# Moving norm sums from TensorE to GpSimd, and one residual stream from TensorE transposes to VectorE squares and GpSimd copies

## The chip, the core and the metric

The kernel runs on one core of a Trainium2 chip. A core has five engines with queues of their own: TensorE (PE in the profile, its weight loads PEld), VectorE (DVE), ScalarE (ACT), GpSimd (POOL) and SyncE (SP), which here issues DMAs. Each engine works through its own queue in order, and waits on semaphores for what others make. The metric is the device time of one execution in microseconds, as the median of the runs. Before the change it is 1138.27 us (three runs, 1137.84 to 1138.35).

## The reference, cut to what matters

A trunk of four pre-norm residual layers over 256 tokens of width 1024, in float32. Layers 0 and 3 mix tokens by differential attention, layer 1 by block attention (with 256 tokens a single causal block), layer 2 by windowed attention with sinks. Each is followed by a squared-ReLU feed-forward of width 4096, and the end is one more norm.

```
h = x
for i in range(4):
    h = h + mixer_i(rms_norm(h, attn_norm_g[i]))
    a = rms_norm(h, mlp_norm_g[i])
    h = h + (maximum(a @ w_up[i], 0) ** 2) @ w_down[i]
return rms_norm(h, final_norm_g)

rms_norm(x, g) = x * rsqrt(mean(x * x) + 1e-6) * g
```

The mean runs over the 1024 features of a token. A factor per token can be pulled out of every product that follows: the kernel multiplies by the gain `g` early and by the root later. For a mixer the factor is `rsqrt(mean)`. For the feed-forward the square of the ReLU turns it into `1 / mean`, which is multiplied in after the down projection.

## The kernel before, in words

The residual stream lies transposed in SBUF: four tiles `hT[j]` of 128 features x 512 (two blocks of 128 features, each with 256 tokens). A float32 product is made of float32r pieces: each operand is split into a high part and a remainder (`whi` by ScalarE, `wlo` by VectorE, L189 and L190; `hg`, `uu`, `oo` in the same way), and three of the four products are added in PSUM. The weights come as 185 pieces of 128x2048, fetched by SyncE up to five pieces ahead and split two pieces ahead of TensorE (`take`). So VectorE's subtraction for a piece stands in its queue between the other work, some two pieces before TensorE needs it.

PSUM has eight banks, four with the tag `wk` (`p_up`, `p_sum`, `p_row`, scores, transposes) and four with `acc` (`p_in`, `p_d`, `p_down`, `p_res`, `p_last`). A group of the up projection (`up_proj`, 16 groups a layer) fills two `wk` banks; VectorE joins each with ScalarE's copy `cross` (L742) and frees it, and the group after next writes it again.

A norm's sum of squares is gathered as the stream is updated: `norm_sum` squares each `hT[j]` on ScalarE and adds on VectorE, which gives `acc`, 128 partitions x 256 tokens (L359). What is left is a sum over the 128 partitions, and TensorE does it with a matrix of ones, in two forms:

- `mean_square` (`p_sum`, L368): `acc` is the stationary operand, so the result has tokens on partitions. It serves the four mixers, through `norm_factor` and the Newton steps of `rsqrt`, whose result `nr` scales the products out of PSUM (L713 for queries and keys), and the last feed-forward, as `factor`.
- `mean_row` (`p_row`, L383): the ones are stationary, so every partition holds all 256 token sums. VectorE scales it to `rowx` and takes the reciprocal into `row` (L948). It serves the feed-forwards of layers 0 to 2, whose down projection leaves features on partitions (`into`, L753).

In the last layer the output must have tokens on partitions. So after group 1 of the up projection (`then`) TensorE transposes the whole stream, 16 blocks of 128x128 into `p_res`, and ScalarE copies it to `res[t]`, 128 tokens x 1024 (L961). `down_out` makes the last down projection in two halves of 512 columns, adds `res` (`close`, L853), and scales by the final norm (`finish`); GpSimd raises to the power -0.5 there (L321).

The order on each engine is made by a planner that lists instructions as it expects them to become ready; on TensorE some instructions are held behind others by hand (`TURNS`: in layers 1 and 3 the first `p_sum` stands behind the 32nd `p_in`). A reader of a result stands at a fixed place in its engine's queue; if the result is late, all that is behind it is late too.

Of the kernel before, what the change touches and what calls it, by code (L numbers as in the profile page):

```python
# [4 lines left out]

# [5 lines left out]

F32 = mybir.dt.float32
F32R = mybir.dt.float32r
I32 = mybir.dt.int32
AF = mybir.ActivationFunctionType
OP = mybir.AluOpType
AX = mybir.AxisListType

P = 128
D = 1024  # L20
S = 256
NT = S // P
# [3 lines left out]
EPS = 1e-6  # L26
# [34 lines left out]
        (("p_s", 16), ("p_in", 168)),  # L61
    ),
    1: (
        (("p_sum", 0), ("p_in", 31)),
        (("p_s", 0), ("p_in", 83)),
        (("p_s", 12), ("p_in", 131)),
        (("p_s", 24), ("p_in", 227)),
# [20 lines left out]
        (("p_d", 150), ("p_d", 161)),  # L88
    ),
    3: (  # L90
        (("p_sum", 0), ("p_in", 31)),
        (("p_s", 0), ("p_in", 83)),
        (("p_s", 12), ("p_in", 131)),
        (("p_s", 24), ("p_in", 225)),
# [52 lines left out]
def trunk(ctx: ExitStack, tc: tile.TileContext, xT, gains, lams, swa_row, fng, weights, out):  # L147
# [8 lines left out]
    def bank(tag, name):  # L156
        return ps.tile([P, 512], F32, tag=tag, name=name, bufs=4)

    def room(j, shape, name, dt=F32):

        return sb.tile(shape, dt, tag=f"slot{j}", name=name, bufs=1)
# [36 lines left out]
    def take():  # L198
        i = used[0]
        used[0] += 1  # L200
        while len(fetched) < min(weights.shape[0], i + FAR + 1):
            fetch()
        while len(staged) < min(weights.shape[0], i + LOOK + 1):
            stage()
        return staged[i]

    def r3(n):
        return lambda t: t.rearrange("p (a b) -> p a b", a=n)
# [153 lines left out]
    def mean_square(n):  # L362

        p = bank("wk", "p_sum")
        for t in range(NT):
            T.matmul(p[:, P * t:P * t + P], n.acc[:, P * t:P * t + P], ones, start=True, stop=True)
        x = tiny.tile([P, NT], F32, tag="nx", name="nx", bufs=1)
        V.tensor_scalar(x, p[:, :S].rearrange("p (t m) -> p t m", m=P)[:, :, 0], 1.0 / D, EPS, op0=OP.mult, op1=OP.add)  # L368
        return x

    def norm_factor(n, by_power):

        x = mean_square(n)
        r = tiny.tile([P, NT], F32, tag="nr", name="nr")
        rsqrt(r, x, NT, by_power)
        return r

    def mean_row(n):

        p = bank("wk", "p_row")  # L380
        T.matmul(p[:, :S], ones, n.acc, start=True, stop=True)
        x = sb.tile([P, S], F32, tag="rowx", name="rowx", bufs=1)
        V.tensor_scalar(x, p[:, :S], 1.0 / D, EPS, op0=OP.mult, op1=OP.add)  # L383
        return x

    def mm3(out, lh, ll, rh, rl, start, stop, **kw):
# [216 lines left out]

    def mixer_layer(i, n):
        mixer, slot = i % 3, i // 3
        r = norm_factor(n, i == 0)
        parts = []
        kpad = new_keys()
        if mixer == 2:
# [223 lines left out]
                    block_step(p, hi[:, k], lo[:, k], us[16 * h + k], h + k == 0, h == 1 and k == 15)  # L833
            into(n, d, p, row)

    def down_out(us, res, factor):

        grow = sb.tile([P, D], F32, tag="raw", name="grow", bufs=RAW)
        nc.sync.dma_start(grow, bcast(fng, D))
        ss = cst.tile([P, 2, NT], F32, name="fss")  # L840
        x = cst.tile([P, 2, NT], F32, name="fx")
        r = cst.tile([P, NT], F32, name="fr")


        given = [sb.tile([P, D], F32, tag=f"hg{t}", name=f"given{t}", bufs=1) for t in range(NT)]

        def close(t, p, c, part, first=0):


            width = p.shape[-1]  # L850
            o, s = slice(t, t + 1), slice(512 * c + first, 512 * c + first + width)
            y = res[t][:, s]
            V.scalar_tensor_tensor(y, p, factor[:, o], y, op0=OP.mult, op1=OP.add)  # L853
            if part is None:
                return
            sq = sb.tile([P, 512], F32, tag="relu", name="sq")
            if s.stop == D:
                V.tensor_tensor_reduce(sq[:, :width], y, y, op0=OP.mult, op1=OP.add, scale=1.0 / D,
                                       scalar=x[:, 0, o], accum_out=x[:, 1, o])
                return  # L860
            A.activation(sq[:, :width], y, AF.Square, accum_out=ss[:, part, o])
            V.tensor_tensor(given[t][:, s], y, grow[:, s], op=OP.mult)

        def finish(t, bound, fresh):

            o = slice(t, t + 1)
            y = r[:, o]
            rsqrt(y, x[:, 1, o], 1, True)
            rows = slice(P * t, P * t + P)
            z = given[t]  # L870
            A.activation(z[:, :bound], z[:, :bound], AF.Copy, scale=y)
            nc.scalar.dma_start(out[rows, :bound], z[:, :bound])
            if bound < fresh:
                s = slice(bound, fresh)
                V.tensor_scalar(z[:, s], z[:, s], y, None, op0=OP.mult)
                nc.sync.dma_start(out[rows, s], z[:, s])
            s = slice(fresh, D)
            V.scalar_tensor_tensor(z[:, s], res[t][:, s], y, grow[:, s], op0=OP.mult, op1=OP.mult)
            nc.sync.dma_start(out[rows, s], z[:, s])

        def sofar(t, parts):
            o = slice(t, t + 1)
            V.tensor_scalar(x[:, 0, o], ss[:, 0, o], 1.0 / D, EPS, op0=OP.mult, op1=OP.add)
            for j in parts:
                V.scalar_tensor_tensor(x[:, 0, o], ss[:, j, o], 1.0 / D, x[:, 0, o], op0=OP.mult, op1=OP.add)

        for c in range(2):
            banks = [bank("acc", "p_last") for _ in range(NT)]
            parts = []

            def last(t, ks, p=None, first=0, alone=False):
                p = banks[t] if p is None else p
                cols = slice(first, first + p.shape[-1])
                for q, k in ks:
                    hi, lo = parts[q]
                    u, s = us[4 * q + k], slice(P * t, P * t + P)
                    mm3(p, u[:, 0, s], u[:, 1, s], hi[:, k, cols], lo[:, k, cols],
                        (q, k) == (ks[0] if alone else (0, 0)), (q, k) == ks[-1] and k == 3 and q > 5,
                        skip_group_check=True)

            for q in range(8):
                parts.append([r3(4)(x) for x in take()])
                if q < 6:
                    for k in range(4):
                        for t in range(NT):
                            last(t, [(q, k)])
            ends = [(q, k) for q in (6, 7) for k in range(4)]
            last(0, ends)
            close(0, banks[0], c, c)
            if c == 0:  # L910
                last(1, ends)
                close(1, banks[1], 0, 0)
                for t in range(NT):
                    sofar(t, [])
            else:
                finish(0, 512, 512)

                last(1, ends[:4])
                close(1, banks[1], 1, None)
                for h in range(2):  # L920
                    p = bank("acc", "p_last")[:, :256]
                    last(1, ends[4:], p, 256 * h, True)
                    close(1, p, 1, 1 + h, 256 * h)
                    if h == 0:
                        sofar(1, [1])
                finish(1, 448, 768)
# [9 lines left out]
    for i in range(DEPTH):  # L936
        T.layer = i
        parts, rest = mixer_layer(i, n)
        n = new_norm(gv[:, 1, i, :])
        (out_proj if i % 3 == 1 else out_proj_all)(parts, n, rest)  # L940
        held = {}

        def then(g):
            if i + 1 < DEPTH:
                if g == 1:
                    x = mean_row(n)
                    held["row"] = sb.tile([P, S], F32, tag="row", name="row", bufs=1)
                    V.reciprocal(held["row"], x)  # L948
            elif g == 1:
                held["factor"] = cst.tile([P, NT], F32, name="factor")  # L950
                V.reciprocal(held["factor"], mean_square(n))

                held["res"] = [room(16 + t, [P, D], f"res{t}") for t in range(NT)]
                for j in range(4):
                    p = bank("acc", "p_res")
                    for t in range(NT):
                        for b in range(2):
                            T.transpose(p[:, S * t + P * b:S * t + P * b + P],
                                        hT[j][:, S * b + P * t:S * b + P * t + P], ident)
                    for t in range(NT):  # L960
                        A.activation(held["res"][t][:, S * j:S * j + S], p[:, S * t:S * t + S], AF.Copy)  # L961

        us = up_proj(n, then)
        if i + 1 < DEPTH:
            n = new_norm(gv[:, 0, i + 1, :])
            down_proj(us, n, held["row"])
        else:
            down_out(us, held["res"], held["factor"])
    T.take_turns(tc)


# [76 lines left out]
```

## Time and profile before

| what | value |
|---|---|
| median of three runs | 1138.27 us |
| profiled execution | 1137.97 us, its span 1136.2 us |
| granted TensorE clock | 0.999 |
| TensorE busy | 1128.4 us, 99% |
| VectorE busy | 826.2 us, 73% |
| ScalarE busy | 659.8 us, 58% |
| GpSimd busy | 13.2 us, 1%, 43 instructions |
| HBM read | 196.52 MB, 174 GB/s over the span |
| last up projection, last down projection | about 950.6 to 1042.5 us, from there to 1129.7 us |

How to read the rows. A row of a timeline has the start in microseconds, the duration, the engine, the line of the kernel, the operation, the tiles written and read (out<-in), the shape and, after x, how many like instructions are merged in the row; in brackets stands how long the engine was idle before it and what ended that. Matmuls overlap in TensorE's pipeline, so a matmul of 0.40 us may start 0.24 us after the one ahead of it: what one costs is the step between starts. A float32 matmul appears as two instructions. The chain of waits goes back from the last instruction to whatever released each step.

### The profile page before, as it was taken

How to read it: one execution, taken by the hardware profiler on the slowest of the kernel's cores; microseconds unless marked ns; L12 is line 12 of the kernel's file. 1: busy time of each engine (PE TensorE's matmuls, PEld its weight loads, DVE VectorE, ACT ScalarE, POOL GpSimd, SP SyncE). 2: the span in 40 equal slices, each digit the busy share in tenths (PEclk: the TensorE clock that was granted, in tenths of full speed). 3: DMA queues.
4: the chain of work that ended last, by engine and by line, in shares of the span. 5: the costliest groups of instructions: out<-in, count | busy, mean ns of one | idle time of the engine just before them, and what ended most of it. 6: DMA issues, size and time to landing. Idle time of an engine off the chain costs nothing.

```text
span 1136.2 us, 17013 instructions
## 1 busy us (share of the span) xinstructions
PE 1128.4 (99%) x6556; PEld 984.3 (87%) x6556; DVE 826.2 (73%) x1586; ACT 659.8 (58%) x1203; POOL 13.2 (1%) x43
## 2 busy tenths in 40 slices
PE   9999999999999999999999999999999999999997
PEld 7889888888888888888899998888888899888886
DVE  8888977656677697776569887765667788777453
ACT  7766666544476666654446765554446767565342
POOL 2000000000000000000000000000000000000000
PEclk9999999999999999999999999999999999999999
DMA  8543555555544345555553346555554434554551
GB/s 332 197 149 116 185 201 194 194 186 186 185 149 148 122 176 200 196 197 186 185 209 112 112 153 218 185 186 190 190 198 140 145 140 166 196 194 168 186 185 37
DMA packets 30464, 198.66 MB, mean 175 GB/s; under 512 B 3504, under 2 KB 5040, under 8 KB 7216
## 3 DMA queue, kind: packets, MB, share of 16 engines
q1 hardware_dynamic: 30096, 197.09, 50.1%
q8 instruction: 51, 0.84, 0.3%
q10 hardware_dynamic: 288, 0.49, 0.1%
q14 instruction: 29, 0.24, 0.1%
HBM read 196.52 MB, written 1.05 MB: 174 GB/s over the span
## 4 chain that ended last, share of the span: by engine, by line
PE 97%; ACT 1%; DVE 1%; issue 0%; DMA 0%; SPq 0%; POOLq 0%; POOL 0%; DVEq 0%
PE p_up L129 31%; PE p_down L129 23%; PE p_in L129 19%; PE p_last L129 7%; PE p_d L129 7%; PE p_s L129 3%; PE p_av L129 2%; PE p_t L132 1%; PE p_qk L132 1%; PE p_e L129 1%; DMA raw<-in_weights 0%; PE p_o L132 0%; ACT whi L189 0%; ACT hg L345 0%; PE p_sum L129 0%
## 5 line engine op out<-in xcount | busy, mean ns | idle before, releaser
L190 DVE TENSOR_TENSOR wlo<-raw,whi 128x1024 fp32r<-128x1024 f32 (+1 forms) x374 | 446.2, 1209 | 198.2 <-ACT whi L189 197.8
L189 ACT ACTIVATE whi<-raw 128x1024 fp32r<-128x1024 f32 (+1 forms) x374 | 383.9, 1046 | 203.5 <-issue 113.9
L129 PE MATMUL p_up<-hg,whi 128*128 128x512 f32 x1024 | 356.2, 394 | 0.0
L129 PE MATMUL p_up<-hg,wlo 128*128 128x256 f32 x1024 | 283.1, 277 | 0.0
L129 PE MATMUL p_down<-uu,whi 128*128 128x512 f32 x768 | 266.4, 394 | 0.0
L129 PEld LDWEIGHTS p_up<-hg,whi 128*128 128x128 f32 x1024 | 191.8, 188 | 44.0
L129 PE MATMUL p_in<-whi,hg 128*128 128x512 f32 (+1 forms) x736 | 213.3, 372 | 0.0
L129 PE MATMUL p_down<-uu,wlo 128*128 128x256 f32 x768 | 212.7, 277 | 0.0
L129 PEld LDWEIGHTS p_up<-hg,wlo 128*128 128x128 f32 x1024 | 192.3, 188 | 0.5
L129 PEld LDWEIGHTS p_down<-uu,whi 128*128 128x128 f32 x768 | 144.0, 188 | 33.4
L129 PEld LDWEIGHTS p_in<-whi,hg 128*128 128x128 f32 x736 | 132.8, 189 | 22.7 <-ACT hg L345 0.4
L129 PEld LDWEIGHTS p_down<-uu,wlo 128*128 128x128 f32 x768 | 144.2, 188 | 0.0
L129 PE MATMUL p_in<-wlo,hg 128*128 128x512 f32 (+1 forms) x368 | 130.1, 368 | 0.1
L129 PE MATMUL p_d<-oo,whi 128*128 128x256 f32 (+1 forms) x416 | 85.5, 296 | 0.0
L821 ACT ACTIVATE uu<-u 128x512 fp32r<-128x512 f32 x64 | 40.5, 632 | 73.4 <-DVE u L819 73.4
L129 PE MATMUL p_last<-whi,uu 128*128 128x512 f32 (+1 forms) x264 | 79.3, 383 | 0.0
L129 PEld LDWEIGHTS p_in<-wlo,hg 128*128 128x128 f32 x368 | 68.9, 189 | 11.5 <-DVE wlo L190 0.5
L741 ACT ACTIVATE cross<-p_up 128x256 f32<-128x256 f32 x128 | 48.0, 375 | 37.4 <-PE p_up L129 35.4
L129 PEld LDWEIGHTS p_d<-oo,whi 128*128 128x128 f32 x416 | 66.5, 191 | 2.1 <-issue 0.2
L345 ACT ACTIVATE hg<-hT,gn 128x256 fp32r<-128x256 f32 x64 | 31.4, 503 | 61.3 <-DVE hT L754 60.9
L456 ACT ACTIVATE e<-ns,nm 128x128 f32<-128x128 f32 (+1 forms) x128 | 56.8, 446 | 13.3 <-DVE nm L453 13.3
L129 PE MATMUL p_d<-oo,wlo 128*128 128x256 f32 x224 | 63.7, 285 | 0.0
(170 smaller groups left out, 1069.4 us busy)
## 6 DMA issues: line engine op xcount, KB each, us to landing
raw<-in_weights SPq DMA_DIRECT2D x181, 1024.0 KB, 4.9
raw<-in_weights SPq DMA_DIRECT2D x8, 256.0 KB, 4.7
raw<-in_weights SPq DMA_DIRECT2D x4, 512.0 KB, 7.2
hT<-in_xT SPq DMA_DIRECT2D x8, 128.0 KB, 4.6
bias<-in_swa_row SPq DMA_DIRECT2D x1, 512.0 KB, 4.3
grow<-in_fng SPq DMA_DIRECT2D x1, 512.0 KB, 3.4
lv<-in_lams SPq DMA_DIRECT2D x1, 256.0 KB, 6.0
out<-given ACTq DMA_DIRECT2D x1, 256.0 KB, 2.8
```

The source lines that it names most:

```text
L129: return self.keep(out.tensor.name.rstrip("_0123456789"), self.engine.matmul(out, *args, **kw))
L132: return self.keep(out.tensor.name.rstrip("_0123456789"), self.engine.transpose(out, *args, **kw))
L189: high = A.activation(hi[:, s], raw[:, s], AF.Copy)
L190: low = V.tensor_tensor(lo[:, s], raw[:, s], f(hi[:, s]), op=OP.subtract)
L345: A.activation(both[:, 0], h, AF.Copy, scale=g)
L456: A.activation(e[:, s], ns[:, s], AF.Exp, bias=nm[:, t:t + 1], scale=-1.0, accum_out=l[:, t:t + 1])
L741: A.activation(cross, p[:, S:], AF.Copy)
L821: A.activation(both[:, :, 0], r3(2)(u), AF.Copy)
```

## The change

Three things are changed.

1. Where `mean_row` and two of the mixers (layers 1 and 3), and the last feed-forward, had a matmul with ones, GpSimd now sums `acc` over the partitions (`partition_all_reduce`); every partition gets all 256 sums. `mean_row` scales that row in place. Where tokens must be on partitions (`mean_column`), VectorE multiplies each 128x128 half of the row with the identity and sums along the row, which picks each partition's own token. The mixers of layers 0 and 2 keep the matmul. The two entries of `TURNS` that placed `p_sum` go.
2. The 16 transposes of the last layer and ScalarE's eight copies go. Instead VectorE transposes `hT` in squares of 32x32 (`turn_stream`, one instruction for each of the four tiles), and GpSimd puts the squares in place with 64 copies of 32 partitions x 128 elements. This stands behind the second and third piece of the last down projection's first half; the buffers `hg2` and `hg3` hold the squares.
3. `res` is made in `down_out` and is no longer handed to it.

In the built program TensorE's order is otherwise the same. GpSimd has two more instructions without operands, ahead of the first sum over partitions and of the last powers.

```diff
-    def norm_factor(n, by_power):
-        x = mean_square(n)
+    def norm_factor(n, by_power, direct):
+        x = mean_square(n) if direct else mean_column(n)
...
+    def sum_row(n):
+        x = sb.tile([P, S], F32, tag="row", name="row", bufs=1)
+        G.partition_all_reduce(x, n.acc, P, ROP.add)
+        return x
+
     def mean_row(n):
-        p = bank("wk", "p_row")
-        T.matmul(p[:, :S], ones, n.acc, start=True, stop=True)
-        x = sb.tile([P, S], F32, tag="rowx", name="rowx", bufs=1)
-        V.tensor_scalar(x, p[:, :S], 1.0 / D, EPS, op0=OP.mult, op1=OP.add)
+        x = sum_row(n)
+        V.tensor_scalar(x, x, 1.0 / D, EPS, op0=OP.mult, op1=OP.add)
+        return x
+
+    def mean_column(n):
+        row = sum_row(n)
+        x = tiny.tile([P, NT], F32, tag="nx", name="nx", bufs=1)
+        for t in range(NT):
+            junk = sb.tile([P, P], F32, tag="junk", name="junk", bufs=1)
+            V.tensor_tensor_reduce(junk, row[:, P * t:P * t + P], ident, op0=OP.mult, op1=OP.add, scale=1.0 / D,
+                                   scalar=EPS, accum_out=x[:, t:t + 1])
         return x
...
-        r = norm_factor(n, i == 0)
+        r = norm_factor(n, i == 0, mixer != 1 and i < 3)
...
+        res = [room(16 + t, [P, D], f"res{t}") for t in range(NT)]
+        def turn_stream(j):
+            z = sb.tile([P, 2, 2, NT, 4, 32], F32, tag=f"hg{2 + j}", name=f"squares{j}", bufs=1)
+            for h in range(2):
+                V.transpose(z[:, h].rearrange("p a t i c -> p (a t i c)"), hT[2 * j + h])
+            for t in range(NT):
+                for i in range(4):
+                    for g in range(4):
+                        to = res[t][32 * i:32 * i + 32, 512 * j:512 * j + 512]
+                        G.tensor_copy(to.rearrange("p (a b c) -> p a b c", a=4, c=32)[:, :, g, :],
+                                      z[32 * g:32 * g + 32].rearrange("p h a t i c -> p (h a) t i c")[:, :, t, i, :])
...
+                if c == 0 and q in (1, 2):
+                    turn_stream(q - 1)
...
-                    x = mean_row(n)
-                    held["row"] = sb.tile([P, S], F32, tag="row", name="row", bufs=1)
-                    V.reciprocal(held["row"], x)
+                    held["row"] = mean_row(n)
+                    V.reciprocal(held["row"], held["row"])
...
-                V.reciprocal(held["factor"], mean_square(n))
-                held["res"] = [room(16 + t, [P, D], f"res{t}") for t in range(NT)]
-                for j in range(4):
-                    p = bank("acc", "p_res")
-                    for t in range(NT):
-                        for b in range(2):
-                            T.transpose(p[:, S * t + P * b:S * t + P * b + P],
-                                        hT[j][:, S * b + P * t:S * b + P * t + P], ident)
-                    for t in range(NT):
-                        A.activation(held["res"][t][:, S * j:S * j + S], p[:, S * t:S * t + S], AF.Copy)
+                V.reciprocal(held["factor"], mean_column(n))
```

More of the change, by code (lines that the diff above doesn't have):

```diff
@@ L7 @@
 import concourse.tile as tile
-from concourse import mybir
+from concourse import bass_isa, mybir
 from concourse._compat import with_exitstack
@@ L16 @@
 OP = mybir.AluOpType
+ROP = bass_isa.ReduceOp
 AX = mybir.AxisListType
@@ L63 @@
     1: (
-        (("p_sum", 0), ("p_in", 31)),
         (("p_s", 0), ("p_in", 83)),
@@ L90 @@
     3: (
-        (("p_sum", 0), ("p_in", 31)),
         (("p_s", 0), ("p_in", 83)),
@@ L834, in down_proj, with down_out @@
             into(n, d, p, row)
-    def down_out(us, res, factor):
+    def down_out(us, factor):
         grow = sb.tile([P, D], F32, tag="raw", name="grow", bufs=RAW)
@@ L967, in trunk @@
         else:
-            down_out(us, held["res"], held["factor"])
+            down_out(us, held["factor"])
     T.take_turns(tc)
```

## The prediction

> **What bounds the kernel now.** I read the page first (span, busy shares, chain of waits), then the timeline of each engine around every instruction that the change touches.
>
> ```profile
> span 1136.2 us, 17013 instructions
> PE 1128.4 (99%) x6556; PEld 984.3 (87%) x6556; DVE 826.2 (73%) x1586; ACT 659.8 (58%) x1203; POOL 13.2 (1%) x43
> PE 97%; ACT 1%; DVE 1%; issue 0%; DMA 0%; SPq 0%; POOLq 0%; POOL 0%; DVEq 0%
> ```
>
> TensorE is busy for 99% of the span and is 97% of the chain. So whatever leaves its queue is gained in full, and whatever makes that queue wait is lost in full. VectorE, at 73%, feeds TensorE through buffers, so the question is how late it may be.
>
> **What TensorE loses.** The order of the changed program is that of before on TensorE, with only these matmuls gone. Their price is not their duration but the step that they add between neighbours.
>
> ```profile
> 129.50 0.28 PE L129 MATMUL p_up<-hg,wlo 128*128 128x256 f32 x1
> ...
> 129.85 0.28 PE L129 MATMUL p_up<-hg,wlo 128*128 128x256 f32 x1
> 129.97 0.59 PE L129 MATMUL p_row<-acc,ones 128*128 128x256 f32 x2
> ...
> 130.63 0.28 PE L129 MATMUL p_up<-hg,wlo 128*128 128x256 f32 x1
> ...
> 302.27 1.07 PE L129 MATMUL p_in<-whi,hg 128*128 128x512 f32 x4
> 303.17 0.62 PE L129 MATMUL p_in<-wlo,hg 128*128 128x512 f32 x2
> 303.63 0.61 PE L129 MATMUL p_in<-whi,hg 128*128 128x512 f32 x2
> 304.08 0.60 PE L129 MATMUL p_sum<-ones,acc 128*128 128x128 f32 x4
> ...
> 304.99 0.62 PE L129 MATMUL p_in<-wlo,hg 128*128 128x512 f32 x2
> ...
> 962.36 0.27 PE L129 MATMUL p_up<-hg,wlo 128*128 128x256 f32 x1
> ...
> 962.91 1.91 PE L132 MATMUL p_res<-ident,hT 128*128 128x128 f32 x16
> ...
> 964.89 0.28 PE L129 MATMUL p_up<-hg,wlo 128*128 128x256 f32 x1
> ```
>
> A pair of `p_up` matmuls has a step of 129.85 - 129.50 = 0.35 us; across `p_row` it is 0.78, so `p_row` costs 0.43, three times: 1.29. From four `p_in` to the next two takes 0.90 (302.27 to 303.17), with `p_sum` between them 1.36 (303.63 to 304.99): 0.46, in two mixers: 0.92. In the last layer `p_sum` and the 16 `p_res` transposes together make 2.53 of a step of 0.35: 2.18. Gain: 1.29 + 0.92 + 2.18 = 4.4 us. ScalarE also loses eight copies of `p_res`; it is no bound (58%), so I count nothing.
>
> **What GpSimd has to do: the unknown T.** No sum over partitions is in the trace. T is the duration of one over 128x256; the nearest rows of GpSimd:
>
> ```profile
> 1.14 0.20 POOL masks.py:197 MEMSET ident<- 128x128 f32 x1
> ...
> 1.74 0.29 POOL masks.py:199 TENSOR_SCALAR_AFFINE_SELECT ident<-ident 128x128 f32<-128x128 f32 x1
> ...
> 18.60 0.71 POOL L321 TENSOR_TENSOR nr<-nx,minus_half 128x2 f32<-128x2 f32 x1 [12.60 <-DVE an L292]
> ...
> 1125.84 0.54 POOL L321 TENSOR_TENSOR fr<-fx,minus_half 128x1 f32<-128x1 f32 x1 [287.10 <-DVE fx L858]
> ```
>
> Lower end: one streamed pass, two affine selects, 0.6 us. Upper end: the power costs 0.71 - 0.54 = 0.17 us per column, so 256 columns take 44 us. Between them: 128 rows need seven halvings, each a pass over 256 columns, at 0.3 us (1.5 memsets) to 0.5 (two selects with one start saved): 2.1 to 3.5 us. An addition is a streamed operation like the select, not a function like the power, so I take T = 2.8, and keep both ends.
>
> [...]
>
> **How late each sum may be.** In the changed program VectorE's queue holds the reader of each sum about where the reader of `p_sum` or `p_row` stood, and everything behind it waits too: weight remainders (`wlo`), joins of `p_up`, ropes.
>
> ```profile
> 303.33 0.43 DVE L359 TENSOR_TENSOR acc<-acc 128x256 f32<-128x256 f32 x1
> 303.68 1.22 DVE L190 TENSOR_TENSOR wlo<-raw,whi 128x1024 fp32r<-128x1024 f32 x1
> ...
> 306.13 0.17 DVE L324 TENSOR_SCALAR nr<-nx 128x2 int32<-128x2 int32 x1
> ...
> 307.90 0.16 DVE L328 SCALAR_TENSOR_TENSOR nr<-nw,nr 128x2 f32<-128x2 f32 x1
> ...
> 310.21 0.43 DVE L421 TENSOR_TENSOR ropea<-qk,cc 128x256 f32<-128x256 f32 x1
> ...
> 311.07 0.43 DVE L426 TENSOR_TENSOR qk<-ropea,ropeb 128x256 f32<-128x256 f32 x1
> ...
> 318.49 0.29 DVE L453 CUSTOM_DVE_ANT_0 ns<-p_s,causal 128x128 f32<-128x128 f32 x1 [0.84 <-PE p_s L129]
> 308.93 1.25 ACT L713 ACTIVATE qk<-p_in,nr 128x512 f32<-128x512 f32 x2
> 313.61 1.03 PE L132 MATMUL p_qk<-ident,qk 128*128 128x128 f32 x8
> ```
>
> Mixer of layer 1 (layer 3 has the same rows 542.95 us later). The summed squares are there at 303.76, GpSimd's sum at 303.9 + T. Then VectorE: two column picks of 0.3 (like the 0.29 row), a `wlo` of 1.2 between them, the root's chain of 1.93 (306.13 to 308.06): `nr` at 307.6 + T, against 308.06 now. Behind it 1.25 of scaled copies and 1.29 of rope (310.21 to 311.50): 310.2 + T. TensorE wants the transposes `p_qk` at 313.61, or 313.15 without `p_sum`. TensorE waits T - 2.9 in each of two mixers.
>
> ```profile
> 126.45 0.42 DVE L359 TENSOR_TENSOR acc<-acc 128x256 f32<-128x256 f32 x1
> ...
> 131.76 0.41 DVE L383 TENSOR_SCALAR rowx<-p_row 128x256 f32<-128x256 f32 x1
> ...
> 137.16 0.75 DVE L742 TENSOR_TENSOR relu<-p_up,cross 128x256 f32<-128x256 f32 x2
> 141.49 0.39 PE L129 MATMUL p_up<-hg,whi 128*128 128x512 f32 x1
> 415.04 0.43 DVE L359 TENSOR_TENSOR acc<-acc 128x256 f32<-128x256 f32 x1
> 419.85 0.59 PE L129 MATMUL p_row<-acc,ones 128*128 128x256 f32 x2
> 417.57 0.42 DVE L742 TENSOR_TENSOR relu<-p_up,cross 128x256 f32<-128x256 f32 x1
> ...
> 422.29 1.75 DVE L948 RECIPROCAL row<-rowx 128x256 f32<-128x256 f32 x1
> ```
>
> Feed-forward of layers 0 and 2: the sum is there at 127.0 + T and read at 131.76, so VectorE is late by T - 4.8. The join at 137.16 frees (at 137.6) a bank that TensorE writes at 141.49, or 141.06 without `p_row`: 3.5 more. TensorE waits T - 8.2. In layer 1 the reader stands further ahead, in front of the join at 417.57. That join follows scaling and reciprocal (0.33 + 1.66) at 417.6 + T and frees a bank that the group after next enters with its second block, eight steps of 0.345 after 419.85, where `p_row` stood: 422.6. TensorE waits T - 4.6. The last layer's reader has a slot like layer 0's, and its next bank is needed 2.2 earlier: about T - 9.
>
> At T = 2.8 no wait is left; at 3.9 the waits are 2.0, at 4.9 they eat the gain, at 5.7 they are 6.7.
>
> **The last layer's stream**, and a row for the rivals:
>
> ```profile
> 1054.57 2.36 DVE L190 TENSOR_TENSOR wlo<-raw,whi 128x1024 fp32r<-128x1024 f32 x2 [3.13 <-ACT whi L189]
> 1064.33 0.39 PE L129 MATMUL p_last<-wlo,uu 128*128 128x512 f32 x1
> 1080.63 0.75 DVE L853 SCALAR_TENSOR_TENSOR res<-p_last,factor,res 128x512 f32<-128x512 f32 x1 [1.99 <-PE p_last L129]
> 18.64 1.23 DVE L190 TENSOR_TENSOR wlo<-raw,whi 128x1024 fp32r<-128x1024 f32 x1
> ```
>
> VectorE turns four tiles of 128x512 (at most 0.75 each, like the 128x512 row at 1080.63: 3.0) where it idles up to 3.1 us per weight piece; a pair of `wlo` done at 1056.93 is first used at 1064.33, 7.4 us in hand. GpSimd then makes 64 copies of 32x128: 0.2 to 0.7 each by its rows, 13 to 45 us from about 1038 on (the up projection's end, 1042.5, less 4.4). The first half of the columns (32 copies, at most 23 us, so 1061) is read at 1080.63 less 4.4, the second 43 us after. Hidden: 0. Were that cover gone, lateness would first use up the `wlo` in hand. [...] I put 0.2 on the start, where weights land just in time.
>
> **Sum.** 1137.97 us (profiled execution: span 1136.2 and 1.8 around it) - 4.4 + 0.2 = 1133.8; the median of the runs is 0.3 above that execution: 1134.1, I say 1134.2.
>
> **Rivals.** *The sum arrives late* (slower): T between 5.7 and 44. It decides from 5.7 on. At T = 9: 2 x 6.1 + 4.4 + 2 x 0.8 = 18.2, so 1152. For it: the power row's price per column, and nothing in the trace moves data between partitions on GpSimd. Against: it is an addition. *Break-even*: T from 3.9 to 5.7, 1136 to 1140. [...]
>
> **Chances.** Forecast (T under 3.9): 0.50. Break-even: 0.10. Late sum: 0.30. Blocking with T from 4 to 6: 0.10. A measurement of this kernel tells 0.2% (2.3 us) from no change, so faster 0.50, same 0.10, slower 0.40. The forecast alone spans 1133.0 to 1136; the range goes on to T = 10 (2 x 7.1 + 5.4 + 2 x 1.8 + 1 = 24.2: 1158), above which I leave under 0.2.
>
> **What would show it.** `p_row`, `p_res` and two of the `p_sum` pairs are gone from TensorE. GpSimd's row for the sum gives T at once. If I am right it is under 3.9 and TensorE goes into the first `p_qk` of layers 1 and 3 without idling; if wrong, TensorE idles there, released by ScalarE's `qhl` or VectorE's `qk`, and VectorE idles before its reader, released by GpSimd. [...] The copies should end before 1076.

## The result

The changed kernel takes 1133.48 us (median of five runs, 1133.25 to 1134.26), the kernel before 1138.27 us beside it (1137.84 to 1138.67). The ratio is 0.996, 95% interval 0.9948 to 0.9971: 4.8 us or 0.4% faster, which is more than the 0.2% that a measurement of this kernel can tell. The prediction was 1134.2.

The page of the changed kernel, its span, busy times and the chain by engine:

```profile
span 1131.4 us, 17032 instructions
...
PE 1123.7 (99%) x6522; PEld 979.5 (87%) x6522; DVE 831.9 (74%) x1599; ACT 657.1 (58%) x1195; POOL 56.8 (5%) x113
...
PE 97%; DMA 1%; issue 0%; SPq 0%; DVE 0%; ACT 0%; POOLq 0%; POOL 0%; DVEq 0%
```

TensorE has 34 instructions and 4.7 us of busy time fewer and is still 97% of the chain; GpSimd has 43.6 us more and is 0% of it. TensorE's matmuls after each place that was changed (timeline of TensorE, the changed kernel):

```profile
130.56 0.28 PE L128 MATMUL p_up<-hg,wlo 128*128 128x256 f32 x1
...
304.44 0.62 PE L128 MATMUL p_in<-wlo,hg 128*128 128x512 f32 x2
...
313.07 1.04 PE L131 MATMUL p_qk<-ident,qk 128*128 128x128 f32 x8
...
960.63 0.28 PE L128 MATMUL p_up<-hg,wlo 128*128 128x256 f32 x1
```

The same matmuls stood at 130.63, 304.99, 313.61 and 964.89 before. So TensorE is 0.07 us ahead behind the first `p_row`, 0.55 behind the first `p_sum`, and 4.26 behind the last layer's transposes, from where it stays so to the end. Matched one by one, the steps are 0.45, 0.48 and 0.48 for the three `p_row`, 0.47 and 0.48 for the two `p_sum`, and 2.18 in the last layer: 4.5 us, against which the start is 0.4 later.

GpSimd's new work (timeline of GpSimd; in brackets how long it had been idle):

```profile
303.87 2.61 POOL L380 PARTITION_ALL_REDUCE row<-acc  x1 [8.11 <-DVE acc L358]
415.02 1.79 POOL L380 PARTITION_ALL_REDUCE row<-acc  x1 [108.54 <-DVE acc L358]
...
845.28 2.62 POOL L380 PARTITION_ALL_REDUCE row<-acc  x1 [8.10 <-DVE acc L358]
957.48 1.79 POOL L380 PARTITION_ALL_REDUCE row<-acc  x1 [109.57 <-DVE acc L358]
1039.64 33.74 POOL L869 COPY res<-squares 32x128 f32<-32x128 f32 x64 [80.37 <-DVE squares L864]
```

A sum over 128 partitions of 256 columns takes T = 1.79 us, and 2.6 in the two mixers. The 64 copies take 33.7 us and end at 1073.4. VectorE beside them (timeline of VectorE):

```profile
127.81 1.73 DVE L189 TENSOR_TENSOR wlo<-raw,whi 128x1024 fp32r<-128x1024 f32 x1
...
303.61 1.22 DVE L189 TENSOR_TENSOR wlo<-raw,whi 128x1024 fp32r<-128x1024 f32 x1
...
306.52 0.29 DVE L395 CUSTOM_DVE_ANT_0 junk<-row,ident 128x128 f32<-128x128 f32 x1 [1.69 <-POOL row L380]
...
312.39 0.42 DVE L439 TENSOR_TENSOR qk<-ropea,ropeb 128x256 f32<-128x256 f32 x1
...
957.89 1.76 DVE L189 TENSOR_TENSOR wlo<-raw,whi 128x1024 fp32r<-128x1024 f32 x1
...
1076.42 0.75 DVE L881 SCALAR_TENSOR_TENSOR res<-p_last,factor,res 128x512 f32<-128x512 f32 x1 [1.97 <-PE p_last L128]
```

Three things are to be seen. VectorE now waits for a sum (1.69 us at 306.52), but TensorE goes into `p_qk` without idling: the rotated `qk` is ready at 312.81 and wanted at 313.07, so 0.26 us is all that is left in hand. The two engines do hold each other up: a `wlo` that starts inside a sum takes 1.73 or 1.76 instead of 1.22, and the mixers' sum, which starts inside the `wlo` of 303.61 to 304.83, ends 1.65 after that `wlo` does. And `close` in the last layer waits for TensorE, not for the copies.

### The profile page after: what moved, and what is told of

Read it like the earlier page. It is cut to its first block, busy times and chain, and to the rows that moved or that the text cites. A ratio compares the mean times of both kernels' runs of the same rounds, so it can differ in the third digit from the quotient of the medians.

```text
span 1131.4 us, 17032 instructions
## 1 busy us (share of the span) xinstructions
PE 1123.7 (99%) x6522; PEld 979.5 (87%) x6522; DVE 831.9 (74%) x1599; ACT 657.1 (58%) x1195; POOL 56.8 (5%) x113
## 3 DMA queue, kind: packets, MB, share of 16 engines
HBM read 196.52 MB, written 1.05 MB: 175 GB/s over the span
## 4 chain that ended last, share of the span: by engine, by line
PE 97%; DMA 1%; issue 0%; SPq 0%; DVE 0%; ACT 0%; POOLq 0%; POOL 0%; DVEq 0%
PE p_up L128 31%; PE p_down L128 24%; PE p_in L128 19%; PE p_last L128 7%; PE p_d L128 7%; PE p_s L128 3%; PE p_av L128 2%; PE p_t L131 1%; PE p_qk L131 1%; DMA raw<-in_weights 1%; PE p_e L128 1%; PE p_o L131 0%; SPq L220 0%; SPq L174 0%; DVE wlo L189 0%
```

## The experiments

**The parts alone.** The theory is that the gain is the sum of what leaves TensorE's queue; the rival, that one part pays for another's loss. In the first kernel GpSimd has only the three feed-forwards' row sums (cut, against the changed kernel):

```diff
-        r = norm_factor(n, i == 0, mixer != 1 and i < 3)
+        r = norm_factor(n, i == 0, True)
...
-                V.reciprocal(held["factor"], mean_column(n))
+                V.reciprocal(held["factor"], mean_square(n))
```

(with the `TURNS` entries and the last layer's stream as before). In the second it has only the two mixers' sums, in the third only the last layer's stream, with all sums on TensorE.

> Only the three feed-forward sums (layers 0 to 2) are on GpSimd; mixers, last factor and the residual stream as before. Step theory (what leaves TensorE is gained in full at the step it adds, and a sum of 1.8 us hides in all three places): TensorE's lag against before is -0.44 at each of the three places, -1.3 in all, so 1138.3 - 1.3 = 1137.0. Blocking theory (VectorE and GpSimd hold each other, and that eats part of the gain): the subtraction beside the sum stretches to 1.7 us and TensorE waits behind it, so under half of the 1.3 is left. If the gain of the change came from its start or its end, TensorE's lag here is 0.

> Only the sums of the mixers of layers 1 and 3 are on GpSimd. Step theory: -0.46 at each, -0.9 in all, 1137.4; the first p_qk of both layers starts without idling, but the rope in front of it ends under 0.5 us ahead of it (in the full change 312.81 against about 313.07). Blocking theory: the sum, held back by the subtraction that began just before it, is 2.6 us instead of 1.8, and if the tolerance of 2.9 is smaller than worked out, TensorE waits at p_qk and the gain is gone.

> Only the last layer's stream is turned by VectorE and GpSimd; all sums stay on TensorE (the last factor's too). Step theory: 2.18 less the 0.46 of p_sum, so -1.7 on TensorE, 1136.6. The 64 copies take some 34 us as in the full change, the subtractions beside them stretch by about 0.1 us a pair, TensorE waits for neither. Blocking theory: the copies cost VectorE more than its idle time and TensorE is slower in the last down projection, so less than 1.7 is left. [...]

Measured, with the kernel before at 1138.52: 1136.61 (ratio 0.9987, 0.9978 to 0.9996), 1137.01 (0.9987, 0.9978 to 0.9996) and 1136.04 (0.998, 0.9971 to 0.9989). So 1.9, 1.5 and 2.5 us, each 0.6 to 0.8 more than expected. Part of that is not TensorE's: from its last matmul to the end of the span it is 6.49 us before and 6.01 to 6.04 in all three kernels and the changed one. Without that 0.46, what is left is 1.45, 1.05 and 2.0, and 4.5 together with 0.46 once is 5.0, about the 4.8 of the whole change. Each interval reaches about 1 us to either side, so this adds up to within a microsecond or two and no closer. No part is a loss that another pays for.

**Each sum three times, and six times.** This makes the unknown T larger without moving anything else, so it shows how late a sum may be.

```diff
-        G.partition_all_reduce(x, n.acc, P, ROP.add)
+        for _ in range(3):
+            G.partition_all_reduce(x, n.acc, P, ROP.add)
```

> The full change with each of the six sums made three times, one behind the other (same result); T is then about 5.4 instead of 1.8. Tolerance theory: in the two mixers the sum must be there by about 306.8 of the span and comes at 306.5 + 3.6 = 310.1, so TensorE waits 3.3 us at p_qk in layers 1 and 3, together 6.7; in the feed-forward of layers 0 and 2 T - 8.2 is below zero and in layer 1 the planner puts the reader further back, so nothing there: 1133.5 + 6.7 = 1140.2. If the mixers have more room than worked out (hidden anyway), the time stays at 1133.5 to 1135. If blocking matters more than the reader's place, the feed-forward places show waits of TensorE as well and the time is over 1143.

> The full change with each of the six sums made six times (same result); T is about 10.8. Tolerance theory: mixers: the planner puts one more subtraction ahead of the reader, so the sum is needed by about 307.9 and comes at 315.5: 7.6 us of TensorE's waiting in each, 15.2; feed-forward of layers 0 and 2: T - 8.2 or somewhat more, 2.6 to 3.5 each; layer 1 and the last factor 1 to 2 each. Together 22 to 26 us, 1155 to 1160. If the engines block each other for the whole of each sum, VectorE gets nothing done between the sums and the feed-forward waits are over 6 us each: over 1165.

Three times: 1144.19 us (ratio 1.0053, 1.004 to 1.0065). Six times: 1179.62 (1.0366, 1.0351 to 1.0381, before at 1138.01). Both are far over the forecast from lateness alone, in the range that was said to speak for blocking. The traces say otherwise. Three sums each, layer 1's mixer (timeline):

```profile
304.40 6.39 POOL L381 PARTITION_ALL_REDUCE row<-acc  x3 [8.10 <-DVE acc L358]
...
310.83 0.29 DVE L396 CUSTOM_DVE_ANT_0 junk<-row,ident 128x128 f32<-128x128 f32 x1 [5.46 <-POOL row L381]
...
317.27 1.94 PE L131 MATMUL p_qk<-ident,qk 128*128 128x128 f32 x8 [3.49 <-DVE qk L440]
```

TensorE stands still for 3.49 us; the prediction's tolerance, T - 2.9, gives 6.39 - 2.9 = 3.49. It is the same in layer 3, and no other wait is over 0.2 us, although the feed-forwards' sums took up to 6.5 us. That is 7.0 of the 10.7 us lost against the changed kernel. Most of the rest is in the rows behind the wait: the eight `p_qk` took 1.94 instead of 1.04. TensorE's clock by stretch (windows of the same kernel: busy time, clock, DMA share, GB/s):

```profile
317.00:320.00 3.00, 2.73 (x11) 0.55 0.28 41
320.00:324.00 4.00, 4.00 (x19) 0.91 0.55 233
```

The granted clock was 0.55 in the first three microseconds after the wait. TensorE comes out 5.3 us later than it went in (0.6 to 5.85 behind the changed kernel), 1.8 more than it waited. By the trace the granted clock is 0.50 for 3.41 us (317.28 to 320.69) behind this wait of 3.49, and back at 1.00 from there.

With six sums the waits of TensorE are these (the view of waits: in total, times, longest):

```profile
PE p_qk L131 <- DVE qk L440: 16.6, 2, 8.3
PE p_up L128 <- DVE relu L756: 12.6, 5, 3.8
```

A single wait in the feed-forward and what comes behind it (timeline, then windows as above):

```profile
145.47 0.50 PE L128 MATMUL p_up<-hg,whi 128*128 128x512 f32 x1 [3.69 <-DVE relu L756]
...
448.63 0.50 PE L128 MATMUL p_up<-hg,whi 128*128 128x512 f32 x1 [1.93 <-DVE relu L756]
...
1018.41 0.50 PE L128 MATMUL p_up<-hg,whi 128*128 128x512 f32 x1 [2.41 <-DVE relu L756]
```

```profile
145.00:149.00 4.00, 3.53 (x14) 0.70 0.74 258
...
448.00:452.00 4.00, 3.10 (x16) 1.00 0.00 0
...
1018.00:1022.00 4.00, 3.59 (x20) 1.00 0.72 254
```

With sums of 12.12 us in layer 0, T - 8.2 gives 3.9 (3.69 seen); in the mixers 12.19 - 2.9 gives 9.3 (8.3 seen; the planner put one more `wlo` ahead of the reader there, 1.2 us that no longer stand behind it); for the last factor 12.12 - 9 gives 3.1 (2.41 seen). In layer 1, 11.52 - 4.6 gives 6.9, and 1.93 and 0.80 are seen. But that reader has another place: with three and with six sums the planner put it two joins further back (timeline of VectorE, six sums, then the changed kernel):

```profile
439.71 0.41 DVE L756 TENSOR_TENSOR relu<-p_up,cross 128x256 f32<-128x256 f32 x1
445.63 0.29 DVE L387 TENSOR_SCALAR row<-row 128x256 f32<-128x256 f32 x1 [5.50 <-POOL row L381]
...
448.17 0.41 DVE L756 TENSOR_TENSOR relu<-p_up,cross 128x256 f32<-128x256 f32 x1
```

```profile
416.85 0.29 DVE L386 TENSOR_SCALAR row<-row 128x256 f32<-128x256 f32 x1 [1.57 <-POOL row L380]
...
418.85 0.36 DVE L755 TENSOR_TENSOR relu<-p_up,cross 128x256 f32<-128x256 f32 x1
```

The join at 418.85, the first behind the reader, is the one at 436.18 with six sums, ahead of it. So the 4.6 is not tested here. Behind the waits of 1.93 and 2.41 us the granted clock stood at 1.00. With the wait of 3.69 it was 0.70 in the mean of 145 to 149, with the 3.77 of layer 2 (to 712.14) 0.65 in the mean of 712 to 716, and with the first of 8.3 (to 330.17) 0.50 from 326 to 334. The waits are 29.2 of some 48 us by which TensorE ends later. The slow clock behind four of them is about 8 (1.8 to 2.2 each). About 10 are a third thing: behind its wait, TensorE runs the rest of each feed-forward 1.9% slower at a granted clock of 1.00 (windows of TensorE, first the changed kernel, then six sums):

```profile
150.00:200.00 50.00, 50.00 (x290) 1.00 0.56 190
```

```profile
150.00:200.00 50.00, 50.00 (x285) 1.00 0.60 207
```

In 50 us it has 285 of its instructions in place of 290, without a wait between them; the matmuls that take 31.31 us in the changed kernel (155.87 to 187.18) take 31.92. The kernel with the feed-forward sums alone shows such a stretch, with no wait ahead, in the profiled execution (1139.55, its slowest). What causes it stays open.

**Reading without anybody waiting.** To separate blocking from lateness, 30 more sums of 128 columns into a scratch tile stand behind the sum of the first three feed-forwards.

```diff
         x = sum_row(n)
+        spare = sb.tile([P, P], F32, tag="junk", name="spare", bufs=1)
+        for _ in range(30):
+            G.partition_all_reduce(spare, n.acc[:, :P], P, ROP.add)
```

> The changed kernel, with 30 more sums over partitions of 128 columns, into a scratch tile that nobody reads, behind each of the three feed-forward layers' sums (layers 0 to 2): some 31 us of GpSimd reading SBUF beside VectorE, with nothing waiting for the result (a sum of 128 columns took 1.07 us when alone in the kernel with halves). That only a late result costs time (lateness): the same as the changed kernel, 1133.5 us within 1 us; VectorE's subtractions are stretched but stay ahead. That GpSimd and VectorE holding each other up costs time by itself (blocking): in those stretches VectorE was busy for about 0.72, its operations on two SBUF operands took 1.7 for 1.22 us (wlo) and 1.58 for 0.68 us (u), so it would need about 1.0 to 1.35 of each 31 us, less the 8 us by which it is ahead: 0 to 3 us a layer, and should it be held for the whole of each sum, more than 10 us a layer: 1137 to 1143, or over 1165.

Measured: 1133.56 us (ratio 0.9965, 0.9953 to 0.9977), the same as the changed kernel. GpSimd read SBUF for over 40 us in each of three layers (timeline), and VectorE paid for it (windows of the three stretches: busy time of PE, PEld, DVE, ACT, POOL; first this kernel, then the changed one):

```profile
670.86 42.03 POOL L388 PARTITION_ALL_REDUCE spare<-acc  x30
```

```profile
127.00:160.00 33.00, 33.00 (x192) 28.82 (x191) 31.30 (x41) 18.00 (x29) 30.42 (x23) 1.00 0.61 213
414.00:448.00 34.00, 34.00 (x197) 29.79 (x197) 30.49 (x39) 18.30 (x30) 30.70 (x24) 1.00 0.52 182
668.00:702.00 34.00, 34.00 (x198) 29.75 (x197) 32.13 (x42) 18.93 (x31) 30.91 (x23) 1.00 0.64 218
```

```profile
127.00:160.00 33.00, 33.00 (x192) 28.84 (x191) 29.03 (x41) 19.33 (x31) 1.81 (x1) 1.00 0.67 227
414.00:448.00 34.00, 34.00 (x198) 29.75 (x198) 28.72 (x41) 20.45 (x33) 1.79 (x1) 1.00 0.57 197
668.00:702.00 34.00, 34.00 (x198) 29.73 (x198) 30.11 (x43) 20.18 (x31) 1.79 (x1) 1.00 0.67 229
```

VectorE is busy 93.9 instead of 87.9 of 101 us, TensorE the whole time in both. Over the whole execution VectorE is busy 841.8 us instead of 831.9. GpSimd pays too: 30 sums of 1.07 us take 42. So the blocking is real, some 3 us of VectorE's time a layer here, and by itself it costs nothing in the feed-forward, where VectorE has that time.

**Late without reading.** Here GpSimd was to write a scratch tile ahead of the two mixers' sums.

```diff
+            spare = sb.tile([P, P], F32, tag="junk", name="spare", bufs=1)
+            G.tensor_copy(spare[:, :1], n.acc[:, :1])
+            for _ in range(25):
+                G.memset(spare, 0.0)
         row = sum_row(n)
```

> The changed kernel, with one column's copy and 25 memsets of 128x128 into a scratch tile ahead of the sum of the two mixers that use GpSimd: GpSimd only writes, but the sum starts about 4 us later (memsets of this size were 0.15 us apart at the kernel's start). Lateness: the sum would end about 3.3 us later (it no longer has to wait for the low part beside it), 0.3 us of it is covered, so TensorE would stand still for about 3.0 us at the first transposes of queries and keys, twice, and if its granted clock drops for 4 us after that, as with three sums, 1.7 us more each: 1142 to 1144 (1139.5 if the clock stays). Blocking by reads: writes cost VectorE nothing, so the time would stay below 1136.

Measured: 1149.35 us (ratio 1.01, 1.0086 to 1.0114). In the built program the memsets came behind the sum, and held up its reader, which writes the same buffer (timeline of layer 1's mixer):

```profile
303.51 1.04 POOL L393 COPY spare<-acc 128x1 f32<-128x1 f32 x1 [8.08 <-DVE acc L358]
...
304.53 2.75 POOL L380 PARTITION_ALL_REDUCE row<-acc  x1
...
307.16 6.60 POOL L395 MEMSET spare<- 128x128 f32 x25
...
313.79 0.29 DVE L400 CUSTOM_DVE_ANT_0 junk<-row,ident 128x128 f32<-128x128 f32 x1 [4.40 <-POOL spare L395]
```

So the reader was 7.3 us later than in the changed kernel (306.52) rather than the 3.3 I had counted on, and the figures of the expectation don't hold. The planner also put ten more `p_in` instructions ahead of `p_qk`. TensorE waited 5.1 us there, until 320.23, and its granted clock was 0.58 in the mean of 317 to 321 and 0.57 of 321 to 325. It ends 14.6 us later than in the changed kernel, 7.3 a mixer. What was added are writes and one read of a single column, and the one `wlo` beside the memsets (308.17) took its usual 1.22 us, so in the mixers lateness is enough for a loss; what the new order adds to it was not separated.

**The copies.** In one kernel each of the 64 copies is made twice. In the other GpSimd sets `res` to a constant in place of each copy.

```diff
-                        G.tensor_copy(to.rearrange("p (a b c) -> p a b c", a=4, c=32)[:, :, g, :],
-                                      z[32 * g:32 * g + 32].rearrange("p h a t i c -> p (h a) t i c")[:, :, t, i, :])
+                        G.memset(to.rearrange("p (a b c) -> p a b c", a=4, c=32)[:, :, g, :], 0.5)
```

> The full change with each of the 64 copies made twice (same result): they take some 67 us instead of 34 and end at about 1107. The first half of the columns is then there at about 1073, before the first close at 1076.4, the second before 1120. If the close waits only for its own columns, as the prediction assumed, nothing is lost: 1133.5. If it waits for all 64, VectorE stands still from 1076 to 1107, the subtractions behind it have 6 to 7 us in hand, and some 20 us are lost: 1153 or more.

> The full change, but the 64 GpSimd copies are replaced by 64 memsets of the same places (the residual stream is left out of the last sum): GpSimd writes as much and reads nothing. [...] The time stays at 1133.5 by either, since TensorE waits for neither.

Measured: 1133.40 us (ratio 0.9957, 0.9941 to 0.9974) and 1133.26 (0.9957, 0.9942 to 0.9972): the copies cost nothing, and nothing when there are twice as many. With double copies (timelines of GpSimd and VectorE):

```profile
1040.33 68.41 POOL L870 COPY res<-squares 32x128 f32<-32x128 f32 x128 [80.37 <-DVE squares L864]
...
1077.12 0.75 DVE L882 SCALAR_TENSOR_TENSOR res<-p_last,factor,res 128x512 f32<-128x512 f32 x1 [1.84 <-POOL res L870]
```

The view names a copy as what `close` waited for at 1077.12. But the first half of the copies, which is all that this `close` reads, ended at 1075.43, and TensorE's matmuls are 0.70 us later here than in the changed kernel, as `close` is (1076.42 there). So it still waits for TensorE. The copies of the second half end at 1108.7 and their reader comes at 1120.6. The kernel with constants doesn't tell reading from writing, since its memsets ran already at 943 to 956 us. It does show what VectorE pays for the copies: between 1036 and 1080 no `wlo` is over 1.24 us without them, and nine take 1.25 to 1.31 in the changed kernel.

**Halves.** Each sum as two sums of 128 columns, to see what of T is fixed.

```diff
-        G.partition_all_reduce(x, n.acc, P, ROP.add)
+        for t in range(NT):
+            G.partition_all_reduce(x[:, P * t:P * t + P], n.acc[:, P * t:P * t + P], P, ROP.add)
```

> The full change with each sum over 128x256 made as two over 128x128. This measures T's two parts. If T is all columns, each half takes 0.9 us and nothing changes: 1133.5. If a sum has a fixed part of half a microsecond, each half takes 1.15 and the pair 2.3: the mixers' readers are 0.5 later at most and TensorE waits 0 to 0.3 in each, 1133.5 to 1134.1.

Measured: 1133.18 us (ratio 0.9963, 0.9948 to 0.9978), the same. A half alone took 1.07 us, the whole 1.79: 0.72 for 128 columns (5.6 ns each) and 0.35 for the instruction. Beside VectorE's operations the two halves took up to 4.93 us (layer 0), far over the 2.3 expected, and TensorE waited for none of them.

**The third mixer too.** The mixer of layer 2 also takes GpSimd's sum.

```diff
-        r = norm_factor(n, i == 0, mixer != 1 and i < 3)
+        r = norm_factor(n, i == 0, i == 0)
```

> The changed kernel, with the sum of the third mixer (layer 2) on GpSimd too. The planner orders about 195 of TensorE's instructions in that layer anew. Gain if the rest is as in the two others: the 0.46 us of that p_sum, so 1133.0. If the new order leaves TensorE waiting for the factor (the sum ends about 2.6 us after it could start): up to 3 us slower, 1136. Likeliest within 0.7 us of the changed kernel.

Measured: 1137.48 us (ratio 0.9998, 0.9989 to 1.0007): 4.0 slower than the changed kernel, a miss. Between the first `p_in` and the first `p_up` of layer 2 TensorE takes 78.1 us in place of 74.3. Two new waits are part of it (view of waits):

```profile
PE p_t L131 <- DVE e L560: 1.4, 1, 1.4
...
PE p_qk L131 <- DVE rest L439: 0.8, 1, 0.8
```

They are 2.2 of 3.8. The second is lateness: from the summed squares to the end of the rope that `p_qk` waits for it is 7.8 us in place of 6.7. The rest wasn't traced. One sum taken from TensorE made the planner order a whole layer anew, and the later factor and the new order together cost more than the 0.46 that it saves.

**The kernel before, once more.**

> The kernel before, profiled a second time. It tells which of the differences at both ends of the span belong to the change: in the first profile of before the time from TensorE's last instruction to the end was 6.49 us, in all eight kernels since it was 6.01 to 6.04, and the weight that the first waits take came 0.4 us earlier than in any of them. If these are chance: 6.03 us at the end here, and a start that lies among the others'. If they come with the change: 6.49 us again, and the early start.

Its time was 1138.30, and its two ends are as in the first profile. The last DMA issue of before, with its span, then the second profile of before, then the changed kernel (page and timeline of SyncE):

```profile
span 1136.2 us, 17013 instructions
...
1132.21 0.43 SPq L879 DMA_DIRECT2D out<-given  x1
```

```profile
span 1136.1 us, 17013 instructions
...
1132.16 0.43 SPq L879 DMA_DIRECT2D out<-given  x1
```

```profile
1127.94 0.43 SPq L907 DMA_DIRECT2D out<-given  x1
```

From there to the end it is 4.0 us in both profiles of before and 3.5 in the changed kernel. So the 0.46 us are not chance; they come with another program. By the records of the trace the difference lies in the closing instructions of GpSimd's queue, after the output's last landing (1134.6 before, 1130.4 in the changed kernel): the clearing of the semaphores and the drain behind it take 0.69 us before and 0.21 in the changed kernel. Why is not settled (with the memsets the end was 6.38 instead of 6.03 after TensorE). The start is less clear: at 25 us TensorE is 0.16 us later in the second profile of before, and 0.04 to 1.25 later in the kernels derived from the changed one.

## Why the prediction was right, point by point

- *What TensorE loses*: 4.4 predicted, 4.5 by the steps, 2.18 of them in the last layer as worked out. That the price of a matmul is the step between its neighbours held to 0.05 us at every place.
- *The start*: +0.2 predicted, +0.4 in the profiled execution (0.16 in the second profile of before, so some of it is chance). No run shows a 0.2 as such: at 25 us the kernels derived from the changed one were 0.04 to 1.25 us later than the first profile of before. *The end*: counted as unchanged, and 0.46 us shorter. This shorter end outweighs the later start, which is luck. 1136.2 - 4.5 + 0.4 - 0.46 = 1131.6, against a span of 1131.4.
- *T*: the mis-sized term. 2.8 was taken, between 0.6 and 44; it is 1.79, below even the 2.1 to 3.5 that seven halvings gave. The choice of the low part of the range was right: 5.6 ns a column is far from the power's 170. How the sum is made inside is not shown, so the working that led to 2.8 is not borne out, and that the true T lay on the harmless side of it was luck.
- *Tolerance of the mixers*, T - 2.9: right to 0.01 us with three sums. But it was right with the blocking in it: the mixers' sum took 2.61, not T, because `wlo` stood in its way. In terms of T alone the tolerance is 2.9 - 0.8 = 2.1. Had T been the 2.8 of the prediction, each mixer would have waited 0.7 us, which the prediction put at 0. It came out because T was smaller, with 0.26 us to spare.
- *Tolerance of the feed-forwards*: 8.2 and 9 held within a microsecond. The 4.6 of layer 1 was not tested: with longer sums the reader stood two joins further back, and there the tolerance is 11.52 - 1.93 = 9.6. In the changed kernel the reader stands in front of the join, as predicted. An estimate from the rows: the wait with six sums was at the matmul that stands at 427.47 in the changed kernel, and the bank of the join at 418.85 is written two bank changes of 2.77 us ahead of that, at 421.92. The join ends at 419.21, so 2.7 us are in hand at T = 1.79: 4.5.
- *The stream*: hidden, as predicted. 64 copies of 0.49 us on average lie inside 0.2 to 0.7 (single ones took up to 1.36), and they end at 1073.4, before 1076.
- *The engines block each other*, a rival at 0.10 with T from 4 to 6: that they hold each other up is measured, a price of it in the feed-forward is not. The `wlo` of 1.73 and 1.76 us in place of 1.22 beside a sum, and the sums of 2.6 in place of 1.79 beside a `wlo`, show it. Beside GpSimd's power of two columns before (18.60 to 19.31) the `wlo` at 18.64 took its usual 1.23. No `wlo` was held for a whole sum (below). And the tolerance of 8.2 held within a microsecond, and 30 idle sums a layer cost nothing, since VectorE had the time.
- *The sum arrives late*, a rival at 0.30: its mechanism is shown by the repeated sums, and it would have been worse than worked out. Waits of 3.49 us and more cost some 1.5 to 2.2 us more each, with the granted clock at 0.50 for a part of it.

## What to carry to other kernels

Where TensorE is 99% busy, a helper matmul or transpose is worth the step between its neighbours, and it can be given to an idle engine if the result's last permissible time, read from the rows of its readers, is later than that engine's worst case, with the hold-up by VectorE counted in. Here a late result cost TensorE more than its lateness in every wait of 3.49 us and more, with the granted clock at 0.50 behind it; behind the waits of 1.93 and 2.41 us the clock stood at 1.00, and none between was measured. Where a planner writes the order, a change of one small operation can cost more than it saves, through the new order and a later result, so compare the order on TensorE first; and a reader's tolerance holds only for the order in which it was read.

## What the runs showed of the hardware that was not expected

- A sum over 128 partitions on GpSimd took 1.07 us for 128 columns and 1.79 for 256; a line through these two is 0.35 us and 5.6 ns a column.
- A `wlo` that started inside a sum came out as if held for only about the first half of it: the one at 127.81, started 0.44 us into a sum of 1.81, ended at 129.54; less its usual 1.22 that is 128.32, some 0.95 us after the sum's start. With three sums, the `wlo` that started 0.07 and 0.78 us into a sum (at 675.16 and 421.62) took 2.10 and 1.39 us: 0.95 us again.
- Behind waits of TensorE of 1.93 and 2.41 us the granted clock stood at 1.00. Behind waits of 3.49 and 3.77 us it was at 0.50 for some 3.4 us, behind those of 5.1 and 8.3 for some 4.2, and behind the one of 3.69 for some 2.4 up to 149: estimates from the means of the windows, with 0.50 and 1.00 as the only two values.
- After a wait in a feed-forward with six sums, and once without one, TensorE ran 1.9% slower to that feed-forward's end, at a granted clock of 1.00. The cause is open.
